# Up-projections of the feed-forwards by two-by-two blocks: seven products of sums of blocks in place of eight

## The chip, the cores and the metric

The kernel runs on one core of a Trainium2 chip. The metric is the device time of one execution in microseconds (us). The kernel before was run three times, and one more execution was taken apart by the hardware profiler; all durations below are read from that profile.

## The reference

A network of two blocks works on 512 tokens of 1024 features. The first block has two layers, each with a mixer (windowed means with grid attention, then an mLSTM) and a gated feed-forward of hidden width 2816, all modulated by a condition vector. The second block has a feed-forward, a mixer (HGRN2 and stick-breaking attention), attention on a memory of 256 rows, and a feed-forward again, with halved residuals around the feed-forwards. There are thus four feed-forwards of one shape:

```
# first block, for layer in (0, 1); mod = silu(c) @ ada_w[layer] + ada_b[layer], in six parts
h = modulate(rms_norm(x), sh2, sc2)
x = x + g2 * ((silu(h @ w1) * (h @ w3)) @ w2)         # w1, w3: 1024 x 2816; w2: 2816 x 1024

# second block, first and last step
h = rmsnorm(x, ffn_norm)
gate, up = split(h @ w_gu)                             # w_gu: 1024 x 5632
x = x + 0.5 * ((silu(gate) * up) @ w_down)
```

The products `h @ w1`, `h @ w3` and `h @ w_gu` are called up-projections here, those with `w2` and `w_down` down-projections.

## The kernel before

Everything is held transposed: features stand on the 128 partitions, the 512 tokens along the row. x is eight tiles of 128x512. All products keep float32's precision by halves: a matrix is split into a rounded high half and the low half that is left, and a product is three matmuls per k-tile, high by high, high by low, low by high (`mm3`, L157 to L161). The split of a weight tile is two instructions: ScalarE copies the high half (L150 is the line of every ScalarE instruction), VectorE subtracts it (L129). Weights come from DRAM on SP's queue in pieces of 256 columns, 1 MB each, into two buffers (`raw`, L169), and each 128 columns of them are split (`wsplit`, L177), 128x1024 elements at a time.

`ffn` (L450 to L493) goes through the 22 hidden tiles in groups of 8, 8 and 6. Per hidden tile there are a gate product and an up product of 24 matmuls each, 512 columns wide, into two of the four PSUM banks "mx". Then silu and the multiplication by the up product (L471, L472; in the second block L474 to L477, where both products are also multiplied by rstd, the up product's on GpSimd), and the result g is split, its high half on GpSimd (L126), its low half on VectorE (L129). After a group its part of the down-projection follows: eight output tiles with 3 matmuls for each hidden tile of the group, added to x by `resid` (L548). After the last group, `after(n)` prepares what comes next, tile by tile: the sum of squares for the next norm, and x times its scale or gain. In the second block the norm's rstd isn't applied to the input but to the outputs.

Beside the first feed-forward run 28 quarters of the modulation vectors of both layers (`ada`, L363): a quarter is 1 MB of weights, eight multiply-adds of 128x256 on VectorE (L377, L379), then two tiny matmuls and an addition. 27 steps of them are issued after each hidden tile. Keys and values of the memory (`mem_kv`) are computed ahead of each of the first two feed-forwards and after the first, as filling while norms are under way; matmuls of the values are L249 to L251. The last two tiles of the last down-projection are done by halves of the tokens (`finish`, L495).

The order of the instructions on each engine is set by a scheduler that lists them by readiness and place in the program; how far ahead it may go is bounded by the pools of buffers (`PH["ffn"]`: banks, and numbers of tiles by name). Each engine runs its list strictly in order and waits on semaphores.

## Time and profile before

| | us |
|---|---|
| median of three runs | 2511.76 |
| the runs | 2508.1, 2511.76, 2512.48 |
| span of the profiled execution (the profile gives no time of it beside the span) | 2508.5 |
| TensorE busy | 2425.9 (97%) |
| VectorE, ScalarE, GpSimd busy | 1485.6 (59%), 913.5 (36%), 452.7 (18%) |

The first feed-forward takes 258 to 633 us of the span, the second 968 to 1327, the third 1327 to 1690, the fourth from some 2135 to the end. In each, stretches of up-projections (some 87 us for a group of 8) and of down-projections (43.5 us for a group of 8) follow each other. The page calls TensorE's matmuls PE and its weight loads PEld; both columns count the same 11538 matmuls, and a load overlaps the matmul before it. A wait is given as the instruction that waited and what released it.

### The profile page before, as it was taken

The numbers are of one execution on the slowest core, as the hardware profiler recorded it, in microseconds if no ns is written. First come the engines' busy times: TensorE is split into PE (matmuls) and PEld (weight loads), VectorE is DVE, ScalarE is ACT, GpSimd is POOL, SyncE is SP. The second block draws the span as 40 slices with busy tenths as digits, with TensorE's granted clock in tenths as the row PEclk, the third lists the DMA queues.
The fourth block names the chain that finished last, engine by engine and source line by source line (L and its number), as shares of the span: only waits on it lengthen the run. The fifth ranks groups of instructions, "written<-read, shape, count | busy, mean of one in ns | idle before, by whom it ended". The sixth has DMA issues, their size and how long they took to land.

```text
span 2508.5 us, 29163 instructions
## 1 busy us (share of the span) xinstructions
PE 2425.9 (97%) x11538; PEld 1989.4 (79%) x11538; DVE 1485.6 (59%) x2133; ACT 913.5 (36%) x1356; POOL 452.7 (18%) x464
## 2 busy tenths in 40 slices
PE   7898999999999899999999999999999999999998
PEld 5567788888788668888888888878888788888886
DVE  7888765745876845333345444465778764544444
ACT  3563322222466734222233222244555544322222
POOL 1324100002212341000012112121011401211113
PEclk9999999999999999999999999999999999999999
DMA  9316464634333224323232323322111321222322
GB/s 302 126 57 216 155 218 135 217 107 145 108 101 104 76 83 135 101 84 111 91 100 85 105 97 101 100 92 84 51 51 51 101 85 51 90 95 98 104 84 84
DMA packets 264594, 274.84 MB, mean 110 GB/s; under 512 B 6381, under 2 KB 257133, under 8 KB 264457
## 3 DMA queue, kind: packets, MB, share of 16 engines
q1 hardware_dynamic: 264456, 272.97, 33.2%
q8 instruction: 91, 1.49, 0.3%
q14 instruction: 47, 0.38, 0.0%
HBM read 267.42 MB, written 5.53 MB: 109 GB/s over the span
## 4 chain that ended last, share of the span: by engine, by line
PE 65%; issue 14%; DVE 12%; POOL 4%; ACT 3%; DMA 1%; SPq 0%; DVEq 0%; POOLq 0%; ACTq 0%
PE ps L160 19%; PE ps L159 19%; PE ps L161 19%; DVE wl L129 2%; POOL g L126 1%; POOL s L477 1%; DVE acc L379 1%; PE ps L251 1%; PE ps L249 1%; PE ps L250 1%; DVE qk L791 1%; PE ps L398 1%; PE ps L714 1%; DMA rb<-rd 1%; ACT wh L150 0%
## 5 line engine op out<-in xcount | busy, mean ns | idle before, releaser
L150 ACT ACTIVATE wh<-raw 128x1024 fp32r<-128x1024 f32 (+1 forms) x392 | 406.8, 1038 | 1261.9 <-PE ps L160 1163.8
L159 PE MATMUL ps<-h,wh 128*128 128x512 f32 x2096 | 828.9, 396 | 1.7 <-ACT h L150 0.8
L161 PE MATMUL ps<-h,wl 128*128 128x512 f32 x2096 | 820.2, 392 | 6.6 <-DVE wl L129 6.6
L160 PE MATMUL ps<-h,wh 128*128 128x512 f32 x2096 | 822.5, 393 | 1.5 <-DVE h L584 1.2
L129 DVE TENSOR_TENSOR wl<-raw,wh 128x1024 fp32r<-128x1024 f32 (+1 forms) x392 | 540.9, 1380 | 137.2 <-ACT wh L150 130.0
L161 PEld LDWEIGHTS ps<-h,wl 128*128 128x128 f32 x2096 | 394.7, 188 | 93.5 <-DVE wl L129 8.6
L160 PEld LDWEIGHTS ps<-h,wh 128*128 128x128 f32 x2096 | 395.0, 188 | 87.1 <-issue 3.9
L159 PEld LDWEIGHTS ps<-h,wh 128*128 128x128 f32 x2096 | 395.3, 189 | 86.5 <-issue 3.6
L159 PE MATMUL ps<-g,wh 128*128 128x512 f32 (+1 forms) x716 | 276.9, 387 | 0.4 <-POOL g L126 0.4
L160 PE MATMUL ps<-g,wh 128*128 128x512 f32 (+1 forms) x716 | 276.3, 386 | 0.4 <-DVE g L129 0.4
L161 PE MATMUL ps<-g,wl 128*128 128x512 f32 (+1 forms) x716 | 276.1, 386 | 0.0
L126 POOL TENSOR_SCALAR g<-s 128x512 fp32r<-128x512 f32 x88 | 94.8, 1077 | 663.5 <-DVE s L472 356.2
L379 DVE SCALAR_TENSOR_TENSOR acc<-araw,cond,acc 128x256 f32<-128x256 f32 x315 | 155.3, 513 | 5.2
L159 PEld LDWEIGHTS ps<-g,wh 128*128 128x128 f32 x716 | 134.5, 188 | 28.3 <-POOL g L126 1.3
L160 PEld LDWEIGHTS ps<-g,wh 128*128 128x128 f32 x716 | 134.5, 188 | 28.1 <-DVE g L129 1.1
L477 POOL TENSOR_TENSOR s<-s,rstd 128x512 f32<-128x512 f32 x44 | 58.3, 1324 | 541.8 <-DVE s L476 541.8
L161 PEld LDWEIGHTS ps<-g,wl 128*128 128x128 f32 x716 | 134.5, 188 | 26.9
L556 DVE SCALAR_TENSOR_TENSOR x<-ps,mod,x 128x512 f32<-128x512 f32 x64 | 47.9, 750 | 139.0 <-PE ps L161 139.0
L476 DVE TENSOR_TENSOR s<-ps,s 128x512 f32<-128x512 f32 x44 | 30.4, 692 | 151.3 <-PE ps L161 151.3
L472 DVE TENSOR_TENSOR s<-ps,s 128x512 f32<-128x512 f32 x44 | 30.4, 692 | 137.8 <-PE ps L161 137.8
L556 DVE SCALAR_TENSOR_TENSOR x<-ps,x 128x512 f32<-128x512 f32 x46 | 31.8, 691 | 116.7 <-PE ps L161 116.7
L301 POOL TENSOR_TENSOR ssq<-ssq,sq 128x512 f32<-128x512 f32 x47 | 69.2, 1473 | 90.3 <-ACT sq L150 90.1
(385 smaller groups left out, 2921.4 us busy)
## 6 DMA issues: line engine op xcount, KB each, us to landing
raw<-in_ffn_w_dram SPq DMA_DIRECT2D x60, 1024.0 KB, 5.1
araw<-in_ada_w_dram SPq DMA_DIRECT2D x48, 1024.0 KB, 6.5
raw<-in_ffn_w_gu_dram SPq DMA_DIRECT2D x44, 1024.0 KB, 5.0
raw<-in_ffn_w_down_dram SPq DMA_DIRECT2D x16, 1024.0 KB, 4.9
raw<-in_w_in_dram SPq DMA_DIRECT2D x14, 1024.0 KB, 4.9
raw<-in_od_w_in_dram SPq DMA_DIRECT2D x12, 1024.0 KB, 5.4
raw<-in_mem_w_kv_dram SPq DMA_DIRECT2D x8, 1024.0 KB
raw<-in_ffn_w_dram SPq DMA_DIRECT2D x8, 768.0 KB, 4.3
```

The source lines that it names most:

```text
L126: nc.gpsimd.tensor_scalar(out=hi, in0=src, scalar1=1.0, scalar2=0.0, op0=ALU.mult, op1=ALU.add)
L129: nc.vector.tensor_tensor(out=lo, in0=src, in1=hi.bitcast(F32), op=ALU.subtract)
L150: r = nc.scalar.activation(out=out, in_=in_, func=func, **kw)
L159: mm(out, wh, xh, start=first, stop=False)
L160: mm(out, wh, xl, start=False, stop=False)
L161: mm(out, wl, xh, start=False, stop=last)
L301: nc.gpsimd.tensor_tensor(out=self.ssq, in0=self.ssq, in1=sq, op=ALU.add)
L379: nc.vector.scalar_tensor_tensor(out=acc, in0=t[:, k], scalar=self.cond[:, k:k + 1], in1=acc, op0=ALU.mult, op1=ALU.add)
L472: nc.vector.tensor_tensor(out=s, in0=pss[1], in1=s, op=ALU.mult)
L476: nc.vector.tensor_tensor(out=s, in0=pss[1], in1=s, op=ALU.mult)
L477: nc.gpsimd.tensor_tensor(out=s, in0=s, in1=rstd, op=ALU.mult)
L556: nc.vector.scalar_tensor_tensor(out=self.x[n], in0=ps, scalar=scale, in1=self.x[n], op0=ALU.mult, op1=ALU.add)
```

## The change

An up-projection of 256 columns is a product of a 256x1024 matrix (transposed weights) with a 1024x512 one (the inputs). Cut both in two each way: the weights into four blocks of 512 rows by 128 columns, the inputs into four of 512 features by 256 tokens. The usual product has eight products of blocks. The change takes Strassen's scheme in Winograd's form: seven products, of blocks and of sums of blocks, which are then added to the four blocks of the output. A product of blocks is 4 k-tiles of 3 matmuls, 256 columns wide.

- The inputs are brought into seven *forms* per pair of k-tiles (k and k+4) once per feed-forward: blocks `b` and `y`, sums `t` and `q` (`lead`, `trail`); `MOV` tells which product takes which. They are made as each tile becomes ready, in place of the split inputs.
- The weights' sums are made per 256 columns by VectorE: two of 128x512 (`usums`, L529, L530, for products 5 and 7) and two more (`usums2`, L546, L547, for 6 and 3). High and low halves of sums and blocks are then made as before: three splits of 1024, one of 512 (`ublocks`: products 1, 2 and 4).
- `uprod` accumulates products in PSUM: 1, then 6 and 7 and 4 in one half of bank "wb"; 5, then 3 in one half of bank "wg", product 2 in its other half. Four intermediate sums are copied out by ScalarE (`ukeep`) after products 5, 1, 6 and 7, so that VectorE can add them (`uout1`: L574, L575; `uout2`: L579).
- `ffn` staggers the units: 5 of this unit, 7 of the previous, 1, 2, 4 of the previous, 6, 3. The first unit of the next group (or feed-forward, `then`) is prepared during the last four tiles of a down-projection.
- In the second block the up product's rstd moves to the residual (`resid`, two VectorE instructions; also in `finish`); the gate's stays (L615, L629, L630). The split of g is on ScalarE and VectorE, no longer on GpSimd.
- The modulation beside the first feed-forward: 11 steps after each unit of the first group alone and 22 after each down-projection tile; a quarter's weights come in two pieces of 512 KB, with two buffers of half the size. The memory's tiles lie in buffers of the feed-forward, so the memory is loaded and split again after the first one. Second and third feed-forward share one phase, and the fourth's phase begins before the output projection of the memory attention.

The rest of the diff takes comments away and renames tiles. Its core:

```diff
-        "ffn": dict(ps=dict(mx=4, ad=1), s=3, g=20, acc=2, araw=2, xp=8),
+        "ffn": dict(ps=dict(wb=2, wg=2, ad=1), hx=11, w13=4, w22=4, sm=1, g=16, s=4, u=3, c=6, araw=2),
...
+        nk = self.adak
+        def piece(k0):
+            t = self.t(shape=[P, nk, 256], tag="araw")
+            nc.sync.dma_start(out=t, in_=w[k0 * P:(k0 + nk) * P, o:o + 256].rearrange("(k p) c -> p k c", p=P))
+            return t
+        ts = [piece(k0) for k0 in range(0, KT, nk)]
...
+    MOV = {1: ("b", 0), 2: ("y", 0), 3: ("y", 1), 4: ("q", 1), 5: ("t", 0), 6: ("q", 0), 7: ("t", 1)}
...
+    def lead(self, y):
+        H = S // 2
+        b = self.form()
+        self.split(y[:, 0:H], b[:, 0:H], b[:, H:S])
+        return dict(b=b, y1=y)
+    def trail(self, f, y):
+        nc, H = self.nc, S // 2
+        y1 = f.pop("y1")
+        def sub(out, a, b):
+            nc.vector.tensor_tensor(out=out, in0=a, in1=b, op=ALU.subtract)
+        def both(key, src):
+            f[key] = (self.form(), self.form())
+            self.split(src, *f[key])
+        t, q = self.t(tag="u"), self.t(tag="u")
+        sub(t[:, 0:H], y1[:, H:S], y1[:, 0:H])
+        sub(t[:, H:S], y[:, H:S], y1[:, H:S])
+        both("t", t)
+        both("y", y)
+        sub(q[:, 0:H], y[:, H:S], t[:, 0:H])
+        sub(q[:, H:S], y[:, 0:H], q[:, 0:H])
+        both("q", q)
...
+    def usums(self, u):
+        nc, v = self.nc, u["raw"]
+        s = u["s"] = self.t(shape=[P, 2, 4, P], tag="sm")
+        nc.vector.tensor_tensor(out=s[:, 0], in0=v[:, 0:4, P:2 * P], in1=v[:, 4:8, P:2 * P], op=ALU.add)
+        nc.vector.tensor_tensor(out=s[:, 1], in0=v[:, 0:4, 0:P], in1=v[:, 0:4, P:2 * P], op=ALU.subtract)
+        h, lo = (self.t(F32R, shape=[P, 2, 4, P], tag="w13") for _ in range(2))
+        self.split(s, h, lo)
+        u[5], u[7] = (h[:, 0], lo[:, 0]), (h[:, 1], lo[:, 1])
+    def ublocks(self, u):
+        v = u["raw"]
+        h, lo = self.wsplit(v[:, :, 0:P])
+        u[1], u[2] = (h[:, 0:4], lo[:, 0:4]), (h[:, 4:8], lo[:, 4:8])
+        u[4] = tuple(self.t(F32R, shape=[P, 4, P], tag="w22") for _ in range(2))
+        self.split(v[:, 4:8, P:2 * P], *u[4])
+    def usums2(self, u):
+        nc, v, s = self.nc, u["raw"], u["s"]
+        nc.vector.tensor_tensor(out=s[:, 0], in0=v[:, 4:8, P:2 * P], in1=s[:, 1], op=ALU.subtract)
+        nc.vector.tensor_tensor(out=s[:, 1], in0=v[:, 4:8, 0:P], in1=s[:, 0], op=ALU.subtract)
+        h, lo = self.wsplit(s.rearrange("p a k c -> p (a k) c"))
+        u[6], u[3] = (h[:, 0:4], lo[:, 0:4]), (h[:, 4:8], lo[:, 4:8])
+    def uprod(self, u, forms, m, ks=range(4)):
+        H = S // 2
+        if m in (1, 5) and 0 in ks:
+            u["wb" if m == 1 else "wg"] = self.ps("wb" if m == 1 else "wg")
+        out = u["wg"][:, H:S] if m == 2 else u["wg" if m in (3, 5) else "wb"][:, 0:H]
+        wh, wl = u[m]
+        mm = self.nc.tensor.matmul
+        for k in ks:
+            xh, xl = self.mov(forms[k], m)
+            mm(out, wh[:, k], xh, start=(m in (1, 5) and k == 0), stop=False, skip_group_check=True)
+            mm(out, wh[:, k], xl, start=False, stop=False, skip_group_check=True)
+            mm(out, wl[:, k], xh, start=False, stop=(k == 3), skip_group_check=True)
+    def ukeep(self, u, m):
+        u["c", m] = self.t(shape=[P, S // 2], tag="c")
+        self.act(out=u["c", m], in_=u["wg" if m == 5 else "wb"][:, 0:S // 2], func=AF.Copy)
+    def uout1(self, u, out):
+        H = S // 2
+        tt = self.nc.vector.tensor_tensor
+        tt(out=out[:, 0:H], in0=u["wg"][:, H:S], in1=u["c", 1], op=ALU.add)
+        tt(out=out[:, H:S], in0=u["wg"][:, 0:H], in1=u["c", 6], op=ALU.add)
+    def uout2(self, u, out):
+        self.nc.vector.tensor_tensor(out=out, in0=u["c", 7], in1=u["c", 5], op=ALU.add)
+        return u["wb"][:, 0:S // 2]
...
+        def out1(u, gs):
+            j = u["j"]
+            if not u["up"]:
+                s = sgs[j] = self.t(tag="s")
+                self.uout1(u, s)
+                if rstd is not None:
+                    nc.vector.tensor_tensor(out=s, in0=s, in1=rstd, op=ALU.mult)
+                self.act(out=s, in_=s, func=AF.Silu)
+            else:
+                v, s = self.t(tag="u"), sgs.pop(j)
+                self.uout1(u, v)
+                nc.vector.tensor_tensor(out=s, in0=s, in1=v, op=ALU.mult)
+                gated(s, j, gs)
...
+                ps = self.uout2(u, s[:, halves[1]])
+                if rstd is not None:
+                    nc.vector.tensor_tensor(out=s[:, halves[0]], in0=ps, in1=rstd[:, halves[0]], op=ALU.mult)
+                    nc.vector.tensor_tensor(out=s[:, halves[1]], in0=s[:, halves[1]], in1=rstd[:, halves[1]],
+                                            op=ALU.mult)
...
+            for i, u in enumerate(us):
+                nxt = us[i + 1] if i + 1 < gn else None
+                fresh = gi == 0 and i == 0
+                if fresh:
+                    for m in (5, 1, 2):
+                        self.uprod(u, forms, m, range(3))
+                self.uprod(u, forms, 5, range(3 * fresh, 4))
+                self.ukeep(u, 5)
+                self.usums2(u)
+                if i + 2 < gn:
+                    self.uload(us[i + 2])
+                if prev:
+                    self.uprod(prev, forms, 7)
+                    self.ukeep(prev, 7)
+                self.uprod(u, forms, 1, range(3 * fresh, 4))
+                self.ukeep(u, 1)
+                if nxt:
+                    self.usums(nxt)
+                self.uprod(u, forms, 2, range(3 * fresh, 4))
+                if prev:
+                    self.uprod(prev, forms, 4)
+                    out2(prev, gs)
+                if nxt:
+                    self.ublocks(nxt)
+                else:
+                    t0 = next(tiles)
+                self.uprod(u, forms, 6)
+                self.ukeep(u, 6)
+                self.uprod(u, forms, 3)
+                out1(u, gs)
+                prev = u
+                if side is not None and gi == 0:
+                    self.some(side, 11)
+            self.uprod(prev, forms, 7)
+            self.ukeep(prev, 7)
+            ps0 = self.ps()
+            self.mms(ps0, t0, gs, 0, 3)
+            self.uprod(prev, forms, 4)
...
+                if then_ and n >= 4:
+                    self.ubegin(then_, n - 4)
                 if side is not None:
-                    self.some(side, 27)
-            def evac(n, ps):
-                self.resid(n, ps, scale)
-                if gi == len(groups) - 1:
-                    after(n)
-            if last and gi == len(groups) - 1:
-                tiles = self.wtiles(w2, 0, D, j0, gn)
-                self.proj(w2, 0, D, gs, evac, tiles=tiles, end=6)
-                last(self.tile6, tiles, gs)
-            else:
-                self.proj(w2, 0, D, gs, evac, k0=j0)
-    def finish(self, tile6, tiles, gs):
-        """the last two tiles of x, the final norm and the output, by halves of the tokens"""
+                    self.some(side, 22)
...
+            nc.vector.scalar_tensor_tensor(out=v, in0=pss[n, h], scalar=0.5, in1=rs[:, half[h]], op0=ALU.mult,
+                                           op1=ALU.mult)
+            nc.vector.tensor_tensor(out=x, in0=x, in1=v, op=ALU.add)
...
+        if rstd is not None:
+            v = self.t(tag="u")
+            nc.vector.scalar_tensor_tensor(out=v, in0=ps, scalar=scale, in1=rstd, op0=ALU.mult, op1=ALU.mult)
+            nc.vector.tensor_tensor(out=self.x[n], in0=self.x[n], in1=v, op=ALU.add)
...
-                    self.mem_kv(ms, ks=range(4, 8))
-        hs = self.ffn2(gain, a["ffn1_w_gu_2"][0], a["ffn1_w_down_2"][0], "mix_norm")
+                    self.mem_kv(self.mem_load(), ks=range(4, 8))
+                else:
+                    self.ss_start()
+                    self.ffn(forms, then, a["ffn1_w_down_2"][0], self.rstd, 0.5, self.normed_next("mix_norm", gain))
```

How this moves instructions is seen in the order on each engine. First, VectorE in the second group of the third feed-forward, before: two hidden tiles (`ps` is a product in PSUM, `raw` the weights as they came, `wh` and `wl` their halves, `s` the gated product, `g` its split).

```order
L474 TENSOR_TENSOR s_10919<-ps_10865,rstd_10035 128x512
L129 TENSOR_TENSOR wl_10929<-raw_10857,wh_10928 128x1024
L476 TENSOR_TENSOR s_10919<-ps_10894,s_10919 128x512
L129 TENSOR_TENSOR wl_10958<-raw_10859,wh_10957 128x1024
L129 TENSOR_TENSOR g_10925<-s_10919,g_10924 128x512
L474 TENSOR_TENSOR s_10986<-ps_10932,rstd_10035 128x512
L129 TENSOR_TENSOR wl_11000<-raw_10995,wh_10999 128x1024
L476 TENSOR_TENSOR s_10986<-ps_10961,s_10986 128x512
L129 TENSOR_TENSOR wl_11029<-raw_10997,wh_11028 128x1024
L129 TENSOR_TENSOR g_10992<-s_10986,g_10991 128x512
```

VectorE in the third feed-forward of the changed kernel, one gate unit with what belongs to its neighbours (`sm` are sums of blocks of weights, `c` products kept by ScalarE):

```order
L575 TENSOR_TENSOR s_13439<-ps_13315,c_13425 128x256
L546 TENSOR_TENSOR sm_13367<-raw_13206,sm_13367 128x512
L615 TENSOR_TENSOR s_13439<-s_13439,rstd_13057 128x512
L547 TENSOR_TENSOR sm_13367<-raw_13206,sm_13367 128x512
L579 TENSOR_TENSOR s_13527<-c_13479,c_13328 128x256
L630 TENSOR_TENSOR s_13527<-s_13527,rstd_13057 128x256
L129 TENSOR_TENSOR wl_13462<-sm_13367,wh_13461 128x1024
L129 TENSOR_TENSOR wl_13533<-raw_13336,wh_13532 128x1024
L529 TENSOR_TENSOR sm_13496<-raw_13336 128x512
L530 TENSOR_TENSOR sm_13496<-raw_13336 128x512
L629 TENSOR_TENSOR s_13527<-ps_13352,rstd_13057 128x256
L129 TENSOR_TENSOR w_2371_13537<-raw_13336,w_2370_13536 128x512
```

Ten rows were two units' worth of work; now a unit has some fourteen, and L579 stands between L547 and the split of what L547 makes.

TensorE in the third feed-forward before: two k-tiles of a gate product (`h` are the split inputs).

```order
L159 MATMUL ps_10865<-h_9814,wh_10861 128x512
L160 MATMUL ps_10865<-h_9815,wh_10861 128x512
L161 MATMUL ps_10865<-h_9814,wl_10862 128x512
L159 MATMUL ps_10865<-h_9847,wh_10861 128x512
L160 MATMUL ps_10865<-h_9848,wh_10861 128x512
L161 MATMUL ps_10865<-h_9847,wl_10862 128x512
```

TensorE in the changed one: product 7 of a unit (bank `ps_13352`), and the first matmuls of product 5 of the next (bank `ps_13444`; `w` are halves of sums of weights, `hx` and `h` are forms).

```order
L561 MATMUL ps_13352<-hx_12905,w_2326_13240 128x256
L562 MATMUL ps_13352<-hx_12906,w_2326_13240 128x256
L563 MATMUL ps_13352<-hx_12905,w_2327_13241 128x256
L561 MATMUL ps_13352<-hx_12956,w_2326_13240 128x256
L561 MATMUL ps_13444<-hx_12905,w_2346_13370 128x256
L562 MATMUL ps_13444<-hx_12906,w_2346_13370 128x256
L562 MATMUL ps_13352<-h_12957,w_2326_13240 128x256
L563 MATMUL ps_13352<-hx_12956,w_2327_13241 128x256
```

The matmuls are half as wide, and two of the next unit's product 5 stand inside product 7 of the unit before.

VectorE after the first feed-forward, ahead of the mLSTM, before: the norm's root (L324), then the inputs of the mLSTM (L432, L434), with weight splits between.

```order
L324 SCALAR_TENSOR_TENSOR rstd_4712<-nv_4717,rstd_4712 128x512
L129 TENSOR_TENSOR wl_4793<-raw_4790,wh_4792 128x1024
L432 TENSOR_TENSOR h_4505<-h_4505,rstd_4712 128x512
L432 TENSOR_TENSOR h_4536<-h_4536,rstd_4712 128x512
L432 TENSOR_TENSOR h_4596<-h_4596,rstd_4712 128x512
L129 TENSOR_TENSOR wl_4825<-raw_4790,wh_4824 128x1024
L434 SCALAR_TENSOR_TENSOR h_4865<-h_4505,mod_85,h_4864 128x512
```

The same place in the changed kernel (L440 and L442 are the inputs, L387 the modulation's multiply-adds):

```order
L324 SCALAR_TENSOR_TENSOR rstd_6210<-nv_6215,rstd_6210 128x512
L387 SCALAR_TENSOR_TENSOR c_6095<-araw_6091,cond,c_6095 128x256
L440 TENSOR_TENSOR h_5893<-h_5893,rstd_6210 128x512
L387 SCALAR_TENSOR_TENSOR c_6095<-araw_6091,cond,c_6095 128x256
L440 TENSOR_TENSOR h_5932<-h_5932,rstd_6210 128x512
L387 SCALAR_TENSOR_TENSOR c_6095<-araw_6091,cond,c_6095 128x256
L442 SCALAR_TENSOR_TENSOR h_6387<-h_5893,mod_85,h_6386 128x512
```

Steps of the modulation that stood beside the feed-forward now stand between the norm and the inputs of the mLSTM.

## Rows read from the trace of the kernel before

**Rows 1.** Page: busy us (share, instructions); busy tenths in 40 slices; granted clock.

```profile
PE 2425.9 (97%) x11538; PEld 1989.4 (79%) x11538; DVE 1485.6 (59%) x2133; ACT 913.5 (36%) x1356; POOL 452.7 (18%) x464
...
PE   7898999999999899999999999999999999999998
...
PEclk9999999999999999999999999999999999999999
```

**Rows 2.** Windows: stretch, length, busy PE, PEld, DVE, ACT, POOL; clock; DMA; GB/s.

```profile
395.40:487.20 91.80, 91.80 (x425) 76.33 (x423) 62.39 (x112) 21.03 (x25) 4.85 (x7) 1.00 0.58 188
...
968.20:1055.00 86.80, 86.80 (x385) 71.85 (x385) 31.77 (x30) 22.90 (x27) 4.34 (x7) 1.00 0.33 107
1055.00:1098.50 43.50, 43.50 (x193) 36.03 (x192) 16.80 (x17) 8.49 (x8) 0.62 (x1) 1.00 0.30 97
1459.60:1546.60 87.00, 87.00 (x385) 72.05 (x384) 43.04 (x39) 21.64 (x24) 19.37 (x14) 1.00 0.30 97
2265.10:2352.10 87.00, 87.00 (x386) 72.03 (x385) 43.02 (x39) 21.65 (x24) 19.36 (x14) 1.00 0.29 97
```

**Rows 3.** Waits of TensorE: total us, how many, longest.

```profile
PE ps L161 <- DVE wl L129: 10.5, 5, 4.0
...
PE ps L251 <- DVE wl L129: 4.0, 1, 4.0
```

**Rows 4.** Timeline, TensorE, memory's products: start, duration; first and last of 26.

```profile
956.34 0.28 PE L249 MATMUL ps<-wh,mh 128*128 128x256 f32 x1
...
959.33 0.28 PE L250 MATMUL ps<-wh,ml 128*128 128x256 f32 x1
```

**Rows 5.** Lines: weight loads of one line, busy and mean ns; idle time before.

```profile
L160 PEld LDWEIGHTS ps<-h,wh 128*128 128x128 f32 x2096 | 395.0, 188 | 87.1 <-issue 3.9 <-DVE h L584 2.9 <-DVE h L129 1.6
```

**Rows 6.** Lines by form, VectorE.

```profile
L129 DVE TENSOR_TENSOR wl<-raw,wh 128x1024 fp32r<-128x1024 f32 x352 | 502.7, 1428 | 132.9 <-ACT wh L150 125.8
L379 DVE SCALAR_TENSOR_TENSOR acc<-araw,cond,acc 128x256 f32<-128x256 f32 x315 | 155.3, 513 | 5.2
...
L476 DVE TENSOR_TENSOR s<-ps,s 128x512 f32<-128x512 f32 x44 | 30.4, 692 | 151.3 <-PE ps L161 151.3
...
L377 DVE TENSOR_SCALAR acc<-araw,cond 128x256 f32<-128x256 f32 x45 | 17.5, 388 | 3.5 <-DMA araw<-in_ada_w_dram 3.5
...
L129 DVE TENSOR_TENSOR v<-ps,v 128x256 fp32r<-128x256 f32 x16 | 6.7, 420 | 3.8 <-ACT v L150 3.8
```

**Rows 7.** Timeline, VectorE: start, duration, instruction, [wait before it and its releaser].

```profile
283.79 1.67 DVE L129 TENSOR_TENSOR wl<-raw,wh 128x1024 fp32r<-128x1024 f32 x1
285.39 0.68 DVE L129 TENSOR_TENSOR g<-s,g 128x512 fp32r<-128x512 f32 x1
...
293.88 0.69 DVE L472 TENSOR_TENSOR s<-ps,s 128x512 f32<-128x512 f32 x1 [3.42 <-PE ps L161]
294.49 0.15 DVE L406 TENSOR_TENSOR mod<-ps,cols 128x2 f32<-128x2 f32 x1
...
1328.33 1.23 DVE L129 TENSOR_TENSOR wl<-raw,wh 128x1024 fp32r<-128x1024 f32 x1 [0.16 <-ACT wh L150]
...
1331.57 0.69 DVE L322 TENSOR_TENSOR nv<-rstd 128x512 f32<-128x512 f32 x1
1332.29 0.69 DVE L323 TENSOR_TENSOR nv<-nv,nv 128x512 f32<-128x512 f32 x1
...
1341.19 2.34 DVE L129 TENSOR_TENSOR wl<-raw,wh 128x1024 fp32r<-128x1024 f32 x1
```

**Rows 8.** Lines by form, ScalarE.

```profile
L150 ACT ACTIVATE wh<-raw 128x1024 fp32r<-128x1024 f32 x352 | 373.0, 1060 | 1160.1 <-PE ps L160 1072.9 <-DVE acc L379 34.6 <-PE ps L250 21.6
...
L148 ACT ACTIVATE s<-s 128x512 f32<-128x512 f32 x44 | 27.8, 631 | 0.3 <-DVE s L474 0.3
...
L150 ACT ACTIVATE mst<-ps 128x256 f32<-128x256 f32 x16 | 5.6, 373 | 13.0 <-issue 10.6 <-PE ps L251 2.1 <-ACT h L150 0.3
```

**Rows 9.** Page: DMA issues of the modulation's weights: KB each, us to landing.

```profile
araw<-in_ada_w_dram SPq DMA_DIRECT2D x48, 1024.0 KB, 6.5
```

More of the change, by code (lines that the diff above doesn't have):

```diff
@@ L437, in modulated, with modulated_forms, gained_form @@
         return hs
+    def modulated_forms(self, layer, which, pres):
+        nc, fs = self.nc, []
+        for k, pre in enumerate(pres):
+            (nc.gpsimd if k in self.modpool else nc.vector).tensor_tensor(out=pre, in0=pre, in1=self.rstd, op=ALU.mult)
+            self.act(out=pre, in_=pre, func=AF.Identity, bias=self.mod_cols(layer, which, k)[0])
+            if k < 4:
+                fs.append(self.lead(pre))
+            else:
+                self.trail(fs[k - 4], pre)
+        return fs
+    def gained_form(self, k, name, fs):
+        y = self.t(tag="s" if k < 4 else "u")
+        self.act(out=y, in_=self.x[k], func=AF.Copy, scale=self.col(name, k))
+        if k < 4:
+            fs.append(self.lead(y))
+        else:
+            self.trail(fs[k - 4], y)
     def gained(self, k, name):
@@ L497, in finish, with mms @@
+    def mms(self, ps, tile, gs, k0, k1):
+        _, wh, wl = tile
+        for k in range(k0, k1):
+            self.mm3(ps, wh[:, k], wl[:, k], *gs[k], k == 0, k == len(gs) - 1)
+    def finish(self, tile6, tiles, gs, rs):
         nc = self.nc
@@ L546, in finish, with resid @@
         normed(1, root(1))
-    def resid(self, n, ps, scale):
+    def resid(self, n, ps, scale, rstd=None):
         nc = self.nc
@@ L1310, in mem_tiles @@
     def mem_tiles(self):
[L1311 to L1312 removed]
+        self.mraw = [self.t(shape=[P, 2, self.N], tag="hx") for _ in range(4)]
+        self.mh, self.ml = ([self.t(F32R, shape=[P, 2, self.N], tag="g") for _ in range(4)] for _ in range(2))
     def mem_norm(self):
@@ L1484, in evac @@
                 self.ss_add(self.x[n])
-                pre1.append(self.mod_pre(layer, 1, n, "xp"))
-            def after(n):
-                self.ss_add(self.x[n])
-                if layer == 0:
-                    pre0.append(self.mod_pre(1, 0, n))
-                else:
-                    gain.append(self.gained(n, "ffn1_norm"))
+                pre1.append(self.mod_pre(layer, 1, n, "g"))
             if layer == 0:
@@ L1503, in run @@
                 w = a["od_w_out"][0]
+            units = self.ffn_units(a["ffn_w1"][layer], 0, a["ffn_w3"][layer], 0)
             with self.phase(**self.PH["ffn"]):
-                side = None
+                self.adak, self.adatag = 4, "c"
+                forms, gain = [], []
+                side, then = None, None
                 if layer == 0:
@@ L1511, in run, with after @@
                     ms = self.mem_load()
+                    then = self.ffn_units(a["ffn1_w_gu_2"][0], 0, a["ffn1_w_gu_2"][0], 2816)
+                def after(n):
+                    self.ss_add(self.x[n])
+                    if layer == 0:
+                        pre0.append(self.mod_pre(1, 0, n))
+                    else:
+                        self.gained_form(n, "ffn1_norm", forms)
                 self.ss_start()
@@ L1530, in run, with normed_next @@
             mix = self.mem_attention(hs, self.rstd)
-        hs = self.resid_proj(a["mem_w_o_2"][0], mix, "ffn2_norm")
-        self.ffn2(hs, a["ffn2_w_gu_2"][0], a["ffn2_w_down_2"][0], None)
-    def ffn2(self, hs, wgu, wd, nxt):
-        rstd, gain = self.rstd, []
-        self.ss_start()
+        with self.phase(**self.PH["ffn"]):
+            forms = []
+            self.resid_proj(a["mem_w_o_2"][0], mix, None, forms=("ffn2_norm", forms))
+            self.ss_start()
+            self.ffn(forms, self.ffn_units(a["ffn2_w_gu_2"][0], 0, a["ffn2_w_gu_2"][0], 2816), a["ffn2_w_down_2"][0],
+                     self.rstd, 0.5, self.normed_next(None, None), last=self.finish)
+    def normed_next(self, nxt, gain):
         def after(n):
@@ L1545, in after, with resid_proj @@
                                              scalar2=0.0, op0=ALU.mult, op1=ALU.add)
-        with self.phase(**self.PH["ffn"]):
-            self.ffn(hs, wgu, 0, wgu, 2816, wd, rstd, 0.5, after, last=None if nxt else self.finish)
-        return gain
-    def resid_proj(self, w, mix, nxt, order=None):
+        return after
+    def resid_proj(self, w, mix, nxt, order=None, forms=None):
         gain = []
@@ L1556, in evac @@
             self.ss_add(self.x[n])
-            gain.append(self.gained(n, nxt))
+            if forms:
+                self.gained_form(n, *forms)
+            else:
+                gain.append(self.gained(n, nxt))
         self.proj(w, 0, D, mix, evac, order=order)
```

165 lines of the change are left out of this document (111 added, 54 removed).

## The prediction

> FF1 and FF2 are the feed-forwards of the first block's two layers, FF3 and FF4 those of the second block. A unit is two output tiles (256 columns) of an up-projection; each feed-forward has 22.
>
> **What bounds the kernel now.** I read the page's busy shares first: TensorE is busy for 97% of the span at full clock, VectorE for 59% [rows 1]. A busy TensorE need not be a full one, so I went to the stretches of the feed-forwards. An up-projection group of FF2 (8 units) takes 86.8 us and holds 385 matmuls, so 0.226 us from one 512-column matmul to the next, with no idle time; VectorE works 32 us of it, ScalarE 23 us [rows 2]. FF3 and FF4 look alike, with 43 us of VectorE. FF1 needs 91.8 us for the same group: it has some 40 matmuls more, those of the modulation done beside it. Over the whole span TensorE waits for a low half of the weights 10.5 us in five waits, longest 4.0, and 4.0 us in one [rows 3]. So every up-projection is bound by how fast matmuls follow each other: 86.8 / 8 = 10.85 us per unit.
>
> **The matmuls.** A unit had 48 matmuls of 512 columns; it gets 7 products x 4 k-tiles x 3 = 84 of 256. Their pitch is in the trace: in the memory's products 26 of them start between 956.34 and 959.33, so 2.99 / 25 = 0.120 us [rows 4]. A half-wide matmul costs 53% of a wide one, and the unit 84 x 0.1196 = 10.05 us. That is 0.80 us less per unit, and 88 x 0.80 = 70 us in all if nothing else is late.
>
> Each of the 84 has its own weight load, and a load lasts 188 ns in the profile [rows 5], longer than the new pitch. The 26 matmuls of [rows 4] also had one each and kept 0.120 us, so loads run side by side under the stream; I count them at nothing. If they went one after the other, a unit would take 84 x 0.188 = 15.8 us, and 88 units 435 us more than before. The Trainium skill (TensorE: Matmul & The Clock Gate; LDWEIGHTS, and The mechanism) gives a load as columns / 1.2 GHz, 107 ns here, and says that it overlaps running matmuls only on another row group; by that a unit would grow from 48 x (213 + 107) ns = 15.4 us to 84 x (107 + 107) ns = 18.0 us. The trace disagrees with its number: 10.85 us for the 48.
>
> **What VectorE gets.** Durations: 1.23 us for a low half of 1024 columns beside nothing on GpSimd, 0.69 for 512, 0.42 for 256 [rows 6, 7]. An instruction that waits for nothing starts about 0.08 us before the end of the one ahead (283.79 + 1.67 against 285.39; 293.88 + 0.69 against 294.49), one that reads its predecessor's result starts after it (1331.57 to 1332.29) [rows 7]. So I take 1.15, 0.61 and 0.34 each. Per unit: three splits of 1024 (3.45), one of 512 and four block sums of 512 (3.05). For the outputs, per gate and up unit together, eight of 256 and three of 512: 4.55, half per unit 2.28. With 0.1 for dependent pairs that is 8.9 us; in FF3 and FF4 the multiplications by rstd add 0.61 + 2 x 0.34 per pair, so 9.5 us. Before it was 32 / 8 = 4 us. What goes is GpSimd's part: its multiplication and split held VectorE up (a low half of 2.34 us at 1341.19) [rows 7].
>
> ScalarE per unit: three copies of 1024 (3.18), one of 512 (0.63), four keeps of 256 (1.49), gate and split 1.26 [rows 8]: 6.6 us of 10.05, no bound by itself, but it stands in VectorE's way: a low half waits for its high half, a keep for TensorE, each in its queue's order.
>
> So VectorE fills 89% (FF1, FF2) and 95% (FF3, FF4) of what TensorE needs, in order, with two waits in each unit: at L579 for a keep of the seventh product, and at the split of the last sums (L547, then ScalarE's 1.06, with only 0.8 of other work between). In FF3 one turn of that queue is 9.5 + 0.3 for the second wait + about 0.5 of ScalarE standing behind its own keeps = 10.3 us; TensorE's row there, with two matmuls of the next unit's fifth product drawn ahead of the seventh, shows how little is left. I take 0.28 us of wait per unit in FF3 and FF4 and 0.15 in FF2: gains of 22 x 0.52 = 11.4 twice and 22 x 0.65 = 14.3. Bounds for the wait: 0 (all covered) to 0.95 (below).
>
> **FF1.** The 28 quarters of modulation still to come, 0.39 + 7 x 0.51 = 4.0 us of VectorE each [rows 6], no longer stand beside all units: 11 of some 21 steps go to each unit of the first group, 22 to each down-projection tile. VectorE there has 8.9 + 2.1 = 11.0 us per unit of the first group against some 10.3, and 1.15 + 0.67 + 4.2 = 6.0 per down tile against 43.5 / 8 = 5.4 [rows 2]. Excess 8 x 0.7 + 16 x 0.6 = 15; some spreads into the next group's units, I take 12. Each quarter's 1 MB now comes in two halves through two half-sized buffers (it took 6.5 us to land [rows 9]), so a quarter may hold VectorE longer; and on SP's queue the weights of the down-projections now stand behind such a half, which waits until VectorE has freed its buffer. Bound 25 in all. TensorE gains 22 x 0.80 = 17.6, so FF1 gains 6 (from -7 to 17).
>
> **The seams.** The forms of the inputs cost VectorE, per pair of k-tiles, four subtractions of 256 and three splits of 512, 3.4 us, where one split of 0.67 stood per k-tile.
> - FF2 to FF3, last four down tiles: 4 x (0.87 + 0.67) + 4 x 3.4 + 2.3 for the next unit's sums = 22 us against 4 x 18 x 0.226 = 16.3 of TensorE; the 27 first products on finished forms cover 3.2, the last form's own chain of about 2.4 comes on top: 5 us lost (0 to 9).
> - Into FF4 the same with wider tiles, 24.7 against 21.7: 3.5 lost (0 to 7).
> - Into FF1 and FF2 the memory's products cover most of the 17 us of forms; before, TensorE already waited 4.0 us there: 2 lost each (0 to 6).
> - After FF1, VectorE's order holds 18 modulation steps between the norm and the last input of the mLSTM, 9 us, half of it under the memory's products: 6 lost (0 to 9). Loading the memory again: 1.
> - The end has one more VectorE instruction per half tile: 0.8.
>
> In all 20 us, so 6 + 14.3 + 2 x 11.4 - 20 = 23 us gained. The profiled execution's span is 2508.5 us; what lies around it isn't given, and the timed runs are 2508.1 to 2512.5, so the median of 2511.8 is 3.3 above it. 2508.5 - 23 + 3.3 = 2489 us.
>
> **Rivals.**
> - The matmuls decide and the rest hides: the 0.3% of waits before shows a program in which little else shows. Gain 70 less 10 for seams: 2452 us. Against it, VectorE at 95%.
> - VectorE's queue decides. If its instructions cost their full durations in this mix, because most read what the one or two before them wrote, a unit is 3 x 1.23 + 5 x 0.69 + (8 x 0.42 + 3 x 0.69) / 2 = 9.9 us, with rstd 10.6, and with 0.4 of uncovered wait 10.3 and 11.0. From 10.85 on a unit loses. FF2 then gains 22 x 0.55 = 12, FF3 and FF4 lose 2 x 22 x 0.15 = 7, FF1 loses 15, the seams 20: 30 us slower, 2542. For it: VectorE's load more than doubles. Against it: the early starts in [rows 7]. The Trainium skill (VectorE: DVE Perf Modes, The DRAIN you can't avoid) says that the next instruction does not start until the pipe is empty, which makes this time; the starts of [rows 7] before the end of the one ahead speak against it for independent instructions.
> - FF1 and the seams eat the gain: FF1 at -7, seams at 35: 2511.8 - 37 + 7 + 35 = 2517, about no change.
> - The change does not shorten TensorE's work: loads that no longer hide behind half as long matmuls, 2508.5 + 435 = 2944 us. Only the pitch of [rows 4] speaks on it, and it speaks against.
>
> **How the numbers follow.** A measurement of this kernel tells 0.2%, 5 us, from no change. My forecast, 2470 to 2506, gets 0.50; the matmuls' time, about 2440 to 2470, 0.15; no change, 2507 to 2517, 0.12; VectorE's queue, 2517 to 2560, 0.21; serial loads 0.02. So faster 0.65, same 0.12, slower 0.23. The range of 8 in 10 leaves out the faster half of the second case and the dearer end of the fourth: 2452 to 2532; the likeliest case's own range is 2470 to 2506.
>
> **What would show it.** Right: an up group of FF2 at 81 to 83 us and of FF3 at 82 to 85 with a VectorE above 80%, 256-column matmuls at 0.120 us, GpSimd all but empty; gaps of TensorE of some us ahead of FF3, FF4 and the mLSTM; first group and down-projections of FF1 waiting on VectorE. Wrong: groups at 88 us or more with waits on the L129 splits in every unit (VectorE's queue), a pitch above 0.13 us, or a granted clock that falls to 1.2 GHz in the feed-forwards because of the waits.

## The result and the profile after

The changed kernel takes 2549.82 us (median of 4 runs, 2548.29 to 2550.78) against 2511.27 before: a ratio of 1.0161, 95% interval 1.0146 to 1.0176. The profiled execution's span grew by 40.5 us, from 2508.5 to 2549.0. The forecast was 2489, and its range ended at 2532.

The page after, to set beside [rows 1]: TensorE is busy for less, the span is longer, and the granted clock is no longer full everywhere.

```profile
PE 2404.5 (94%) x14706; PEld 2109.3 (83%) x14706; DVE 1948.2 (76%) x3147; ACT 1260.3 (49%) x2064; POOL 306.5 (12%) x342
...
PE   7898898989799988999998999999999999999997
...
PEclk9999898999899989999999999999999999999999
```

Where the 40.5 us came from is read off the start of the same event in both traces: the first matmul of each feed-forward, the mLSTM's first product, the second mixer's first product.

| stretch | before, us | after, us | difference |
|---|---|---|---|
| up to FF1 | 258.4 | 258.9 | +0.5 |
| FF1 | 374.3 | 403.9 | +29.6 |
| from FF1's last matmul to the mLSTM's first | 19.3 | 32.9 | +13.6 |
| mLSTM, its output projection, memory's values | 316.2 | 316.8 | +0.6 |
| FF2 | 361.3 | 354.5 | -6.8 |
| FF3 | 362.1 | 363.0 | +0.9 |
| second mixer, memory attention | 444.0 | 446.2 | +2.2 |
| FF4 to the end | 372.9 | 372.8 | -0.1 |

So 43 us are lost in and just behind FF1, and FF2 to FF4, where 17.6 us each were to be had, give 6 in all. The windows after answer to [rows 2] (columns as there): first and second group of FF1 (ups), first and second of FF2, first and second of FF3, the first of FF4, and FF1 whole up to the mLSTM.

```profile
258.90:361.60 102.70, 94.32 (x699) 89.25 (x699) 96.48 (x178) 59.33 (x102) 0.00 (x0) 0.92 0.41 131
408.70:505.20 96.50, 87.68 (x690) 86.58 (x689) 77.81 (x127) 48.07 (x82) 0.00 (x0) 0.93 0.39 123
1012.50:1104.00 91.50, 87.86 (x684) 85.95 (x683) 77.58 (x120) 54.39 (x93) 0.00 (x0) 0.94 0.33 106
1146.20:1225.50 79.30, 79.30 (x662) 79.30 (x661) 64.87 (x97) 47.12 (x79) 0.00 (x0) 1.00 0.32 101
1367.00:1463.60 96.60, 89.64 (x685) 86.16 (x684) 83.59 (x134) 56.30 (x91) 0.00 (x0) 0.96 0.28 90
1506.30:1585.60 79.30, 79.30 (x662) 79.30 (x661) 70.21 (x110) 46.45 (x75) 0.00 (x0) 1.00 0.32 102
2176.20:2269.80 93.60, 89.31 (x686) 85.83 (x685) 84.30 (x136) 53.66 (x88) 0.00 (x0) 0.96 0.28 94
258.90:695.70 436.80, 393.97 (x2590) 360.94 (x2590) 372.47 (x648) 191.14 (x302) 30.93 (x23) 0.93 0.49 154
```

The second groups of FF2 and FF3 run 662 matmuls in 79.30 us, 0.120 each, without a gap: there the scheme gives what the matmuls promise (with the products still open at its end, such a group of 8 takes 82.6 us). The first group of every feed-forward takes 91 to 103 us, with VectorE at 85 to 94%. And FF1 with the join holds 372 us of VectorE; before it was 244:

```profile
258.40:652.00 393.60, 389.64 (x1795) 324.53 (x1794) 244.02 (x397) 98.01 (x115) 42.46 (x41) 0.99 0.49 161
```

TensorE's waits over the whole span, to set beside [rows 3]: the longest sum is that of the modulation's small matmuls (L406) for VectorE's multiply-adds (L387).

```profile
PE ps L406 <- DVE c L387: 31.1, 12, 13.7
PE ps L161 <- DVE wl L129: 14.1, 12, 3.8
...
PE ps L561 <- ACT h L150: 7.7, 6, 2.2
...
PE ps L562 <- DVE h L129: 6.3, 7, 3.0
```

The longest of them stands in TensorE's timeline behind FF1: the four small matmuls of a quarter are next in its order, with the memory's keys behind them, and VectorE is 13.66 us late.

```profile
671.39 0.28 PE L160 MATMUL ps<-g,wh 128*128 128x256 f32 x1
671.74 0.58 PE L406 MATMUL ps<-tabs,c 128*128 128x1 f32 x4
672.18 0.36 PE L161 MATMUL ps<-g,wl 128*128 128x256 f32 x1
686.20 0.98 PE L406 MATMUL ps<-tabs,c 128*128 128x1 f32 x4 [13.66 <-DVE c L387]
687.04 0.56 PE L159 MATMUL ps<-g,wh 128*128 128x256 f32 x1
```

### The profile page after: what moved, and what is told of

The parts are those of the page before. It is cut to its first block, busy times and chain, and to the rows that moved or that the text cites. A ratio compares the mean times of both kernels' runs of the same rounds, so it can differ in the third digit from the quotient of the medians.

```text
span 2549.0 us, 37194 instructions
## 1 busy us (share of the span) xinstructions
PE 2404.5 (94%) x14706; PEld 2109.3 (83%) x14706; DVE 1948.2 (76%) x3147; ACT 1260.3 (49%) x2064; POOL 306.5 (12%) x342
## 4 chain that ended last, share of the span: by engine, by line
PE 69%; DVE 18%; ACT 5%; issue 4%; DMA 3%; POOL 1%; DVEq 0%; SPq 0%; ACTq 0%; POOLq 0%
PE ps L561 11%; PE ps L563 11%; PE ps L562 11%; PE ps L161 9%; PE ps L160 9%; PE ps L159 9%; DVE wl L129 3%; DVE c L387 2%; DMA araw<-in_ada_w_dram 1%; ACT wh L150 1%; DMA raw<-in_ffn_w_dram 1%; DVE h L129 1%; PE ps L249 1%; PE ps L251 1%; PE ps L250 1%
## 5 line engine op out<-in xcount | busy, mean ns | idle before, releaser
L129 DVE TENSOR_TENSOR wl<-raw,wh 128x1024 fp32r<-128x1024 f32 (+1 forms) x304 | 367.8, 1210 | 65.3 <-ACT wh L150 62.1
L161 PE MATMUL ps<-g,wl 128*128 128x512 f32 (+1 forms) x780 | 300.3, 385 | 9.9 <-DVE wl L129 9.9
L160 PE MATMUL ps<-g,wh 128*128 128x512 f32 (+1 forms) x780 | 297.2, 381 | 0.0
L159 PE MATMUL ps<-h,wh 128*128 128x512 f32 x688 | 278.5, 407 | 1.7 <-ACT h L150 0.8
L160 PE MATMUL ps<-h,wh 128*128 128x512 f32 x688 | 274.9, 400 | 1.5 <-DVE h L824 1.2
L161 PE MATMUL ps<-h,wl 128*128 128x512 f32 x688 | 271.7, 397 | 4.3 <-DVE wl L129 4.3
L150 ACT ACTIVATE c<-ps 128x256 f32<-128x256 f32 (+1 forms) x376 | 140.8, 383 | 231.0 <-PE ps L563 223.4
L562 PE MATMUL ps<-h,w 128*128 128x256 f32 x792 | 226.7, 286 | 6.3 <-DVE h L129 6.3
L561 PE MATMUL ps<-h,wh 128*128 128x256 f32 x792 | 229.1, 290 | 2.0 <-ACT c L150 2.0
L562 PE MATMUL ps<-h,wh 128*128 128x256 f32 x792 | 228.5, 289 | 0.0
L563 PE MATMUL ps<-h,wl 128*128 128x256 f32 x792 | 228.3, 288 | 0.0
L161 PEld LDWEIGHTS ps<-g,wl 128*128 128x128 f32 x780 | 149.4, 191 | 42.4 <-DVE wl L129 15.4
L561 PE MATMUL ps<-h,w 128*128 128x256 f32 x616 | 176.1, 286 | 7.7 <-ACT h L150 7.7
L561 PE MATMUL ps<-hx,wh 128*128 128x256 f32 x616 | 178.9, 291 | 2.9 <-ACT hx L150 1.7
L563 PE MATMUL ps<-hx,wl 128*128 128x256 f32 x616 | 177.2, 288 | 3.3 <-DVE wl L129 3.2
L562 PE MATMUL ps<-hx,wh 128*128 128x256 f32 x616 | 176.1, 287 | 0.1
L563 PE MATMUL ps<-h,w 128*128 128x256 f32 x616 | 175.4, 285 | 0.0
L160 PEld LDWEIGHTS ps<-g,wh 128*128 128x128 f32 x780 | 149.4, 192 | 27.5 <-issue 1.3
L161 PEld LDWEIGHTS ps<-h,wl 128*128 128x128 f32 x688 | 130.6, 190 | 36.6 <-DVE wl L129 6.2
```

What stands on the lines that cost most here:

```text
L129: nc.vector.tensor_tensor(out=lo, in0=src, in1=hi.bitcast(F32), op=ALU.subtract)
L150: r = nc.scalar.activation(out=out, in_=in_, func=func, **kw)
L159: mm(out, wh, xh, start=first, stop=False)
L160: mm(out, wh, xl, start=False, stop=False)
L161: mm(out, wl, xh, start=False, stop=last)
L561: mm(out, wh[:, k], xh, start=(m in (1, 5) and k == 0), stop=False, skip_group_check=True)
```

## The experiments

**Is the loss FF1's?** Theory A: in FF1 VectorE has about as much to do as TensorE, and each waits for the other. Rival B: all entries and the clock.

```diff
-self.ffn(lambda: self.modulated_forms(layer, 1, pre1), units, ...)
+if layer == 0:
+    self.ffn_1(lambda: self.modulated(layer, 1, pre1), ...)   # ffn, pools and memory tiles of before
+else:
+    self.ffn(lambda: self.modulated_forms(layer, 1, pre1), units, ...)
```

> The first feed-forward (FF1) in the scheme of before, the other three in the changed one. Theory A (the loss sits in FF1, where VectorE has the modulation beside the sums of blocks and TensorE then waits for it): FF1 up to the mLSTM's first product takes some 394 us instead of 437, and the time falls from 2549.8 by 43 to about 2507 us, 4 us below before. Rival B (the loss is that of the waits at the entries of every feed-forward and of the clock that falls there): less than half of the 43 comes back, 2530 us or more.

Measured: 2505.71 us; to before 0.9985, interval 0.9976 to 0.9995. All 44 us are back, and FF1 with the join (its stretch up to the mLSTM's first product) takes 395.4 us. The edit also takes back the half-sized buffers of the modulation, the place of its steps and the second load of the memory, so it shows where the loss sits and not yet what causes it. What is left of the change, in three feed-forwards, is worth 0.15%.

**Amount or place?** VectorE's multiply-adds of the modulation were cut from eight to two per quarter, in the changed kernel and in the one before.

```diff
-            else:
+            elif self.few == 0 or k == 4:
                 nc.vector.scalar_tensor_tensor(out=acc, in0=tk, scalar=self.cond[:, k:k + 1], in1=acc,
```

> The changed kernel, with six of the eight multiply-adds of each modulation quarter beside FF1 left out (all loads, matmuls and additions stay). That is 28 x 6 x 0.40 = 67 us of VectorE. Theory A (VectorE has more work in FF1, 381 us, than TensorE, 356): TensorE's waits for the modulation's sums (34 us) and most of the clock falls of FF1 go, 2500 to 2512 us. Rival C (not VectorE's amount of work but the half-sized buffers and the place of the steps: the weights of the modulation land late, or TensorE meets the small matmuls too early): 2530 us or more.

> The kernel before, with the same six of eight multiply-adds of each quarter beside FF1 left out. Theory A: VectorE was not the bound there, 2503 to 2511 us. If 67 us of VectorE also counted before, the time would fall below 2495.

Measured (one execution each): 2515.15 and 2507.27 us. The changed kernel gets 35 us faster, the one before 1.4, less than one execution can tell. FF1 with the join and FF1's second group, in the changed kernel with few multiply-adds:

```profile
260.50:650.90 390.40, 378.24 (x2591) 349.86 (x2589) 289.83 (x469) 187.00 (x295) 26.18 (x22) 0.98 0.53 170
406.90:486.60 79.70, 79.70 (x663) 79.56 (x663) 65.53 (x101) 46.45 (x79) 0.00 (x0) 1.00 0.38 119
```

With 83 us less on VectorE the stretch is 46 us shorter and the second group runs as those of FF2 and FF3. Some 8 us of the 46 are lost again just behind it, where the mLSTM's first products wait (4.2 us in one wait for VectorE's `h`). The time is 3 us over the range expected of theory A: the first group still takes 100.1 us, which is the entry's part (below).

Three experiments on the place, with the amount left as it is. First, the modulation's transfers on another queue:

```diff
-            nc.sync.dma_start(out=t, ...)
+            (nc.gpsimd if nk < KT else nc.sync).dma_start(out=t, ...)
```

> The changed kernel with the modulation's weights of FF1 issued from GpSimd's queue, so that neither they nor the feed-forward's weights stand behind each other on SP's. Rival C in its form 'SP's queue': the 5 us transfers on the chain of FF1 go, 2520 to 2535 us. Theory A: the transfers are late only because VectorE frees their buffers late, so 2543 to 2552.

Measured (one execution): 2561.74 us, 12 slower, outside both ranges. FF1 itself started 11 us later, because the quarters ahead of it use the same code; from its first matmul to FF2's it took 754.0 us, against 753.6. VectorE's waits for these weights in FF1 rose from 7.6 to 23.8 us. So leaving SP's queue did not bring them earlier; whether standing behind each other there cost anything, the run does not say.

```diff
-                if side is not None and gi == 0:
-                    self.some(side, 11)
+                if side is not None:
+                    self.some(side, 8)
...
-                    self.some(side, 22)
+                    self.some(side, 17)
```

> The changed kernel with the modulation's steps spread: 8 after each unit of all three groups and 17 after each down-projection tile, in place of 11 after the units of the first group alone and 22. Theory A (amount): VectorE's 372 us of work in FF1 stay against TensorE's 367, with no slack either engine waits for the other, so little comes back: 2535 to 2550 us. Rival D (place: the steps stand in the wrong stretches): FF1 gets near 390 us, 2500 to 2515.

```diff
+        if self.pend:
+            self.ada_sum(*self.pend)      # small matmuls and addition of the quarter before
+        self.pend = (layer, part, quarter, acc)
```

> The changed kernel with each modulation quarter's two small matmuls and their addition issued one quarter (some 13 us) later, out of accumulators of their own, so that TensorE does not stand at them while VectorE is still adding. Rival D in its form 'TensorE meets the small matmuls too early': the 34 us of waits at L406 and the clock falls go, 2505 to 2515 us. Theory A: VectorE is as late as before, and the waits move to the splits of the weights: 2533 to 2548 us.

Measured (one execution each): 2535.29 and 2539.62 us, both in the range of theory A, the first at its edge. Spread, FF1 with the join is 416.9 us with VectorE still at 364:

```profile
260.90:677.80 416.90, 386.16 (x2585) 355.14 (x2585) 364.30 (x640) 188.11 (x298) 32.28 (x23) 0.96 0.51 161
```

With later sums the waits at the small matmuls fell from 29.2 to 10.6 us in that stretch, and new ones came where VectorE and ScalarE are late (in this kernel's lines L426 are the small matmuls, L161 the down-projections, L598 the up-projections, L160 the mLSTM's products):

```profile
PE ps L426 <- DVE ac L443: 10.6, 7, 2.0
PE ps L161 <- DVE wl L129: 6.0, 1, 6.0
PE ps L598 <- ACT hx L150: 5.5, 1, 5.5
PE ps L160 <- DVE h L479: 4.1, 1, 4.1
```

So a better order alone gave back 10 to 15 us, and less work for VectorE in the old order 35. The two overlap, and the runs do not divide the 43 between them.

**What bounds the entries of the others?** After the waits there the granted clock falls: it is 0.94 to 0.96 over the first groups above, where [rows 2] had 1.00. Theory E: the clock is the price. Rival F: VectorE's forms are. The next three experiments keep FF1 as before, so they stand against 2505.71.

```diff
+            if fill and k:
+                for i in range(fill):      # 8, ahead of k-tiles 1 to 3 of the first product
+                    mm(pf[:, 0:H], wh[:, 0], b, start=(i == 0), stop=(i == fill - 1), ...)
```

> FF1 in the scheme of before, and at the entries of the other three feed-forwards 24 extra matmuls of 256 columns each (2.9 us per entry, results unused) put ahead of the products that wait for the inputs' forms. Theory E (the waits at the entries let the granted clock fall, and the slow matmuls cost as much again): the falls at the entries go, 2 to 3 us per entry come back, 2497 to 2503 us. Rival F (VectorE's forms set the end of the entry whatever TensorE does meanwhile): 2504 to 2512 us.

Measured: 2504.36 us, ratio 0.9983 (0.9973 to 0.9993), not told apart from 0.9985. That is in F's range, but only just, so the traces have to decide. First group of FF3 without the extra matmuls, then with them:

```profile
1324.10:1420.80 96.70, 89.73 (x684) 86.25 (x683) 83.55 (x134) 56.30 (x91) 0.00 (x0) 0.95 0.28 89
```

```profile
1324.50:1419.60 95.10, 90.89 (x709) 87.64 (x708) 83.47 (x134) 56.33 (x91) 0.00 (x0) 0.98 0.28 91
```

The stretch at the low level (a granted clock of 0.5, which is 1.2 GHz) shrank from 10.2 to 3.4 us in FF2 and in FF3 and stayed at 6.8 in FF4. The first groups took 91.4, 95.1 and 94.1 us against 91.3, 96.7 and 92.3. That the extra matmuls' own time ate up what the clock gave back would fit these lengths too; the waits speak against it. Without the extra matmuls, then with them, a late wait at FF2's entry (for the high half of the weights' second sums) and the last one for a form at FF3's:

```profile
980.65 0.58 PE L562 MATMUL ps<-hx,wh 128*128 128x256 f32 x1 [0.41 <-ACT wh L151]
1335.54 0.58 PE L563 MATMUL ps<-h,w 128*128 128x256 f32 x1 [2.96 <-DVE h L130]
```

```profile
980.95 0.39 PE L567 MATMUL ps<-hx,wh 128*128 128x256 f32 x1 [0.80 <-ACT wh L151]
1335.95 0.39 PE L568 MATMUL ps<-h,w 128*128 128x256 f32 x1 [2.40 <-DVE h L130]
```

Counted from the feed-forward's first matmul (969.72 and 1324.07, then 970.00 and 1324.49), these waits end after 10.93 and 11.47 us, then after 10.95 and 11.46: the same, whatever TensorE did meanwhile. Theory E is not borne out for FF2 and FF3 (0.1 us lost and 1.6 gained, where it gave 2 to 3 each); in FF4, where the extra matmuls did not shorten the fall, it was not tested.

```diff
-            nc.vector.tensor_tensor(out=out, in0=a, in1=b, op=ALU.subtract)
+            nc.gpsimd.tensor_tensor(out=out, in0=a, in1=b, op=ALU.subtract)
```

> FF1 in the scheme of before, and the four subtractions of each form pair on GpSimd in place of VectorE (16 x 0.34 = 5.4 us less VectorE per entry). Rival F (the amount of VectorE's work bounds the entries): 3 to 5 us per entry at FF3 and FF4 come back, 2495 to 2500 us. Against it: GpSimd takes longer for one and slows VectorE beside it, 2504 to 2512 us.

Measured: 2510.97 us, ratio 1.0010 (1.0001 to 1.0019): worse, in the range of the case against F. The commonest form of the subtraction takes GpSimd 1.08 us on average, where VectorE took 0.41, and VectorE's instructions beside it get longer:

```profile
1330.88 0.68 DVE L530 TENSOR_TENSOR sm<-raw 128x512 f32<-128x512 f32 x1
1331.48 1.22 DVE L130 TENSOR_TENSOR h<-u,h 128x512 fp32r<-128x512 f32 x1
1332.62 1.22 DVE L531 TENSOR_TENSOR sm<-raw 128x512 f32<-128x512 f32 x1
```

That neither proves nor refutes F: over FF2's last down-projections and FF3's first group VectorE's busy time fell from 110.3 to 108.2 us in place of the 5.4 hoped for, and that stretch from 130.0 to 128.9, while from FF3's last down-projections to the end of FF4's first group it took some 4 us longer. The last experiment takes the forms out of the entry instead.

```diff
+            if gi == 0:
+                hs = [f[key] for key in ("b", "y") for f in forms]     # split inputs, 512 wide
+                for jj in range(2):
+                    for u in us[0:2]:
+                        wh, wl = u.pop("w0", None) or self.wsplit(u["raw"][:, :, jj * P:jj * P + P])
+                        ...
+                        self.mmk(ps, wh, wl, hs)
+                        self.trail(forms[2 * jj + u["up"]])            # sums t and q of one form pair
```

> FF1 in the scheme of before; in the other three the first two of the 22 units are plain products of 512 columns on the split inputs, the differences t and q of the inputs are made on VectorE beside them (some 2.6 us per form pair), and the other 20 units are as in the changed kernel. Theory F (VectorE's forms set the end of the entries): the first groups take 82.6 + 1.6 us in place of 91, 97 and 92, so some 28 us come back less 1 to 2 us of new waits in each, 2478 to 2486 us. Rival G (the work only moves: VectorE has 22.5 us for the 21.7 of the two plain units, and TensorE waits at the third): 2490 to 2505 us. If the entries are bound by something else than the forms, 2505 or more.

Measured: 2478.18 us (2477.57 to 2478.74), ratio 0.9866, interval 0.9849 to 0.9882. The first groups of FF2, FF3 and FF4 (the window of FF4 begins 1.3 us behind its first matmul), with the clock at full:

```profile
963.80:1047.90 84.10, 84.10 (x609) 79.96 (x609) 69.02 (x106) 49.37 (x80) 0.00 (x0) 1.00 0.35 112
1310.50:1398.10 87.60, 86.53 (x612) 80.75 (x611) 79.60 (x125) 56.26 (x87) 0.00 (x0) 1.00 0.31 99
2112.00:2197.40 85.40, 85.03 (x607) 80.04 (x608) 77.72 (x124) 52.12 (x83) 0.00 (x0) 1.00 0.31 102
```

They took 91.3, 96.7 and 92.3 us, so 22 of the 28.7 us by which the span is shorter come from here.

Most of the rest does not come from the edit as far as the traces show: 1.5 us lie ahead of FF1 and 4.2 between the mLSTM's first product and FF2's, where both kernels do the same work and the waits ahead of FF2 are the same (2.0 and 2.3 us); between 870 and 900 us the granted clock was at its lower level for twice 3.4 us here and for twice 6.8 there. That the time lies at the lower edge of F's range is thus in part luck; the first groups of FF3 and FF4 stayed 3.4 and 2.5 us above the 84.2 that F gave them.

This experiment takes away the forms, the waits and the falls of the clock together; with the waits above, which the clock did not move, theory F holds for the entries, in the form that making the forms and the weights' sums beside them sets their end. This version beats both kernels, the one before by 1.3%.

## Why the prediction was wrong

- **The matmuls** (right). 84 of them at 0.120 us: 79.30 us for 662. Their weight loads took 198 ns each in the new trace and ran in the matmuls' shadow, as [rows 4, 5] had it. The Trainium skill (TensorE: Matmul & The Clock Gate, The mechanism) says in one sentence that a load overlaps running matmuls only on another row group; this trace does not agree. (The same section names a background weight buffer as a second case.)
- **VectorE's waits in every unit** (0.15 in FF2, 0.28 in FF3 and FF4; too dark). They are there on VectorE, 0.59 us at the split of the second sums, but cost TensorE nothing. VectorE's work was sized rightly: from one L530 to the next but one (1519.56 to 1539.60, two units of FF3) it is busy for 18.8 us, 9.4 a unit, where I had 9.5, and in FF2 8.9, as forecast. What was mis-sized is the wait: I added 0.3 us and 0.5 for ScalarE behind its own keeps, and there are 0.59. So VectorE's turn, 9.4 + 0.59 us, just fits the 10.05 of TensorE.

```profile
1519.56:1539.60 20.04, 20.04 (x169) 20.04 (x168) 18.83 (x31) 12.09 (x21) 0.00 (x0) 1.00 0.34 107
```

```profile
1524.96 0.68 DVE L547 TENSOR_TENSOR sm<-raw,sm 128x512 f32<-128x512 f32 x1
1525.56 0.68 DVE L620 TENSOR_TENSOR s<-s,u 128x512 f32<-128x512 f32 x1
1526.83 1.23 DVE L129 TENSOR_TENSOR wl<-sm,wh 128x1024 fp32r<-128x1024 f32 x1 [0.59 <-ACT wh L150]
1527.98 0.68 DVE L129 TENSOR_TENSOR g<-s,g 128x512 fp32r<-128x512 f32 x1
```

  The early starts of [rows 7] hold in the mix too (1524.96 + 0.68 against 1525.56), and with them falls the rival of VectorE's full durations (10.6 us a unit). The Trainium skill (VectorE: DVE Perf Modes, The DRAIN you can't avoid) has each instruction wait for an empty pipe, but adds that one that is not held starts earlier; the rival and its sentence in the prediction left that out, and these starts agree with the addition. The rival's 2542 us lay near the measured time for a reason that isn't there.
- **FF1** (the failed step). I booked an excess of VectorE over TensorE per stretch, 12 us, bound 25, and so a gain of 6. VectorE's share per unit was about right (8.9 us in FF1's second group, behind its first units); the sum over the whole of FF1 was never made. It is 372 us of VectorE against some 366 of TensorE (22 x 10.05 + 528 x 0.227 + 96 x 0.120 for the memory's keys, and 28 quarters at 0.5 us, from the 5.0 us that ten of them cost in [rows 2]), in two queues that wait for each other. Measured: 29.6 us lost, and 13.6 behind it, where I had 7 for the mLSTM's start and the memory together; the place was the one named, modulation steps between the norm and the mLSTM's inputs. Against the forecast for FF1, its entry and the join (3 us lost) that is 40 of the 63.5 us by which the span was missed; FF2 to FF4 gave 6 where 26 were forecast.
- **The seams** (mis-sized). The forms at the entries of FF3, FF4, FF1 and FF2 were to cost 5, 3.5, 2 and 2 us (for FF4 the working of FF3 would have given 24.7 - 21.7 - 3.2 + 2.4 = 2.2). Against the 82.6 us that a group of 8 takes otherwise, the first groups of FF2, FF3 and FF4 lost 8.8, 13.9 and 10.8, beyond the bounds of 6, 9 and 7; FF1's lost 17.5 even with few multiply-adds, some 2 of them the modulation's own small matmuls. I let the ready products cover 3 us and counted the last form's chain at 2.4. In the trace VectorE works from 1354 to 1375.8 with no pause above 0.44 us, and in its order weight splits and sums of the next units stand between the forms. The last one stands worst: its high half is there at 1375.06, but its low half (the `h` at 1377.71) comes behind two steps of the norm's root, the second of which waits 1.29 us for ScalarE, and TensorE waits 2.96 us for it. From the last tile of x (1370.33) to that low half it takes 8.1 us in place of 2.4:

```profile
1369.59 0.74 DVE L796 SCALAR_TENSOR_TENSOR x<-ps,mod,x 128x512 f32<-128x512 f32 x1
...
1370.85 0.41 DVE L501 TENSOR_TENSOR u<-u,u 128x256 f32<-128x256 f32 x1
1371.18 0.68 DVE L129 TENSOR_TENSOR h<-u,h 128x512 fp32r<-128x512 f32 x1
1371.79 1.22 DVE L129 TENSOR_TENSOR wl<-sm,wh 128x1024 fp32r<-128x1024 f32 x1
1372.92 0.68 DVE L129 TENSOR_TENSOR h<-u,h 128x512 fp32r<-128x512 f32 x1
...
1375.13 0.68 DVE L321 TENSOR_SCALAR nv<-ps 128x512 f32<-128x512 f32 x1
1377.10 0.69 DVE L322 TENSOR_TENSOR nv<-rstd 128x512 f32<-128x512 f32 x1 [1.29 <-ACT rstd L145]
1377.71 0.68 DVE L129 TENSOR_TENSOR h<-u,h 128x512 fp32r<-128x512 f32 x1
...
1378.45 0.55 PE L562 MATMUL ps<-h,w 128*128 128x256 f32 x1 [2.96 <-DVE h L129]
```

- **Rivals.** The one that came nearest is "FF1 and the seams eat the gain", with -7 and 35 where the traces show -43 for FF1 with its join and 33.5 for the other three first groups alone.

What stays open: the 13 us or so of FF2 to FF4 that neither the first groups nor the gain of 6 account for (small waits at the down-projections, ahead of the second mixer and at the end, not followed up), how the 43 us of FF1 divide between amount and order (10 to 15 came back by order alone, in two experiments that were not combined), whether putting the norm's root behind the last form would have been worth its 3 us at FF3's entry, and the entry of FF1 itself, which was not tried with plain units.
